# Moving operands split into even and odd tokens, read in turn from both halves

## The chip, the cores and the metric

The kernel runs on one core of a Trainium2 chip. The metric is the device time of one execution in microseconds (us). Before the change three executions took 2588.56, 2589.22 and 2593.65 us, with a median of 2589.22.

The engines are named as in the profile: PE is TensorE (its matmuls) and PEld its weight loads, DVE is VectorE, ACT is ScalarE, POOL is GpSimd, and SP issues most of the DMAs.

## The reference

One layer of a hybrid decoder runs for a prompt of 256 tokens and 8 sample tokens, 264 tokens in all, width 2048. All data is float32. Cut to what matters here:

```python
proj = x @ w_in                        # 2048 -> 15392 columns
z, xbc, dt, sc_b, sc_c, sc_h, g_a, g_b = split(proj)
y_a = ssd_branch(z, xbc, dt, ...)      # causal conv, chunked scan, gated RMS norm
y_b = sc_b * dwconv3(sc_c * sc_h)      # short gated conv
mix = sigmoid(g_a) * (y_a @ w_branch_ssd) + sigmoid(g_b) * (y_b @ w_branch_sc)
x1 = layer_norm(ALPHA * x + mix @ w_out)
# peer: 8 heads, each picks 16 of 16384 experts by product keys
q = x1 @ peer_wq
idx, gate = top-16 per head
hid = gelu(x1 . peer_u[idx])
x2 = layer_norm(ALPHA * x1 + sum(gate * hid * peer_v[idx]))
y = x2 + sigmoid(x2 @ ple_gate_w) * (p @ ple_proj_w)
```

The time goes into products of a weight matrix with the 264 tokens. For the experts the kernel multiplies 208 of the tokens with all 16384 rows of `peer_u` and `peer_v` (the picks are a mask of gates), and gathers rows for the other 56.

## The kernel before

**Layout.** Activations are held transposed: a tile has 128 features as partitions and the tokens as columns, so a product over 2048 features is a sum over 16 tiles (`kb`). The weights are the stationary operand, 128x128 at a time; the tokens are the moving operand and stream through. Results land in PSUM in the order in which the moving columns were read.

**Three products for float32.** Every operand is cut into a high part, rounded to the matmul's input type (float32r), and a low part, the rest. `half_mm` (lines 242 to 244) then adds high weight x high token, high x low and low x high into the same PSUM columns. Weights arrive by DMA in tiles of 128x2048 (`w`, three buffers). ACT makes the high part of each half (`whi`, line 158) and DVE the low part (`wlo`, line 159).

**Column blocks.** `col_block` makes 128 output features of all tokens: two halves of 8 tiles, 48 matmuls of 264 columns. After each half it runs background tasks (`tick`). There are 200 such blocks: 24 for xbc, 48 for the short conv, 16 for z, 32 for each of the two gated branches with their gates, 16 for `w_out`, 16 for the peer queries and 16 for the ple gate. The last two kinds read 266 columns: behind the tokens lie a column of the norm's scale and one of its offset, so that the norm can be applied after the product (`Norm`, tiles `r1` and `r`).

**Pairs.** For the experts, `pair_block` holds the high and low part of 208 tokens in one tile of 416 columns. The high weights meet all 416 at once (lines 278 and 281), the low weights only the first 208 (line 279). So a 128x128 piece of weights costs one wide and one narrow matmul. There are 128 such blocks for `peer_u` (moving tiles `x1`) and 128 for `peer_v` (moving tiles `co`).

**Who makes the moving tiles.** `split_later` (lines 229 and 230) cuts the outputs of the branches (`yb`, `ya`) and their mix (`mx`). `split_x` cuts the input, `Norm.gather` and `Norm.rest` the inputs of the two later col blocks with a norm, `Norm.parts` the 416-wide `x1`, and `prep` (lines 1432 and 1433) the coefficients `co`. Each is one ACT and one DVE instruction per tile. `xsum` (line 1010) adds the two parts of x for the residual, and `residual` (line 1478) copies the `x1` pairs into the accumulators of the second experts' product.

**Order.** Every engine works through its instructions in the order written by the Python program; there is no scheduler. Background work is put between halves by the credits that a task yields.

Of the kernel before, what the change touches and what calls it, by code (L numbers as in the profile page):

```python
# [10 lines left out]
F = mybir.dt.float32  # L11
# [9 lines left out]
T = PT + NS  # L21
# [30 lines left out]
def hybrid_step(ctx: ExitStack, tc: tile.TileContext, xT, pT, w_in, w_dt, w_bs, w_bc, w_o, w_q, w_pg, w_pp,  # L52
# [165 lines left out]
    def run_out(tk):  # L218
        while tk in tasks:
            tick(1e9)  # L220

    def split_later(src, name, new, hs, ls):
        h = new(name + "h", R)
        l = new(name + "l", R)
        hs.append(h)
        ls.append(l)

        def parts():
            ac.copy(h, src)
            ve.tensor_tensor(l, src, h.bitcast(F), OP.subtract)  # L230

        soon(parts)
        return h, l
# [3 lines left out]
    def half_mm(ps, i, kbs, xh, xl, first, last, m=128):  # L237
        hi, lo = his[i], los[i]
        n = len(kbs)
        for q, kb in enumerate(kbs):  # L240
            wh, wl = hi[:, q * 128:q * 128 + m], lo[:, q * 128:q * 128 + m]
            te.matmul(ps, wh, xh[kb], start=(first and q == 0), stop=False)  # L242
            te.matmul(ps, wh, xl[kb], start=False, stop=False)  # L243
            te.matmul(ps, wl, xh[kb], start=False, stop=(last and q == n - 1))  # L244

    def next_half():
        i = pos["i"]
# [20 lines left out]
    def pair_block(xp, evac, budget):  # L268

        ps = psum.tile([128, 512], F, name="mm", tag="mm", bufs=4)[:, :2 * TD]  # L270
        for half in range(2):
            i = next_half()
            hi, lo = his[i], los[i]
            for q in range(8):
                kb = half * 8 + q
                ws = slice(q * 128, q * 128 + 128)
                if kb < KB - 1:
                    te.matmul(ps, hi[:, ws], xp[kb], start=(kb == 0), stop=False)  # L278
                te.matmul(ps[:, :TD], lo[:, ws], xp[kb][:, :TD], start=False, stop=False)  # L279
                if kb == KB - 1:  # L280
                    te.matmul(ps, hi[:, ws], xp[kb], start=False, stop=True)  # L281
            done_half(i)
            if half == 1:
                evac(ps)
            tick(budget)
# [80 lines left out]
    def dt_mm(k0, k1):  # L366
        for kb in range(k0, k1):
            sl = slice(kb * 32, kb * 32 + 32)
            te.matmul(psd[:32, :T], wdh[:, sl], x_h[kb], start=(kb == 0), stop=False)
            te.matmul(psd[:32, :T], wdh[:, sl], x_l[kb], start=False, stop=False)  # L370
            te.matmul(psd[:32, :T], wdl[:, sl], x_h[kb], start=False, stop=(kb == KB - 1))


    wps = bank("warm")
# [467 lines left out]
    class Norm:  # L842
# [24 lines left out]
        def gather(self, s):  # L867

            j = len(self.d)
            w = self.w  # L870
            beside = w < T
            ve.tensor_tensor(s[:, :w], s[:, :w], self.c[:, :w], OP.subtract)
            self.d.append(s[:, :T])
            h, l = self.new(self.name)
            q = s[:, w:2 * w] if beside else block("dsq")

            def on_act():
                ac.activation(h[:, :w], s[:, :w], AF.Copy, scale=col(self.g, j))
                ac.activation(q, s[:, :w], AF.Square)
                gp.tensor_copy(h[:, T:], self.gb[0][:, j])  # L880
                gp.tensor_copy(l[:, T:], self.gb[1][:, j])
                if j == 0:
                    if beside:
                        a = lp.tile([128, 2, w], F, name="da", tag="as", bufs=2)
                        gp.tensor_copy(a.rearrange("p a t -> p (a t)"), s)
                        self.acc = [(a[:, 0], a[:, 1])]
                        self.both = a.rearrange("p a t -> p (a t)")
                    else:
                        a = block("da")
                        gp.tensor_copy(a, s)  # L890
                        self.acc = [(a, q)]

            def on_dve():
                ve.scalar_tensor_tensor(l[:, :w], s[:, :w], col(self.g, j), h[:, :w].bitcast(F), OP.mult, OP.subtract)
# [12 lines left out]
        def rest(self, xs, sq):  # L907
# [19 lines left out]
            for j in range(16):  # L927
                while self.n <= j:
                    yield ("w", 1)
                h, l, x = self.h[j][:, w:T], self.l[j][:, w:T], xs[:, j]  # L930
                ac.activation(h, x, AF.Copy, scale=col(self.g, j))
                gp.tensor_copy(self.d[j][:, w:], x)
# [56 lines left out]
        def parts(self, xp):  # L989
            for j in range(16):  # L990
                d = self.normal(j, ve)
                pr = pair("x1")
                h, l = pr[:, 0:TD], pr[:, TD:2 * TD]
                xp.append(pr[:, 0:2 * TD])

                def split(d=d, h=h, l=l, j=j):
                    ac.copy(h, d[:, :TD])
                    ve.tensor_tensor(l, d[:, :TD], h.bitcast(F), OP.subtract)
                    gp.tensor_copy(x1sp[:, j], d[:, TD:])

                soon(split)
# [411 lines left out]
    def prep(c):  # L1413

        for k in range(4 * c, 4 * c + 4):
# [16 lines left out]
            ac.copy(co[:, :, 0], al)  # L1432
            ve.tensor_tensor(co[:, :, 1], al, co[:, :, 0].bitcast(F), OP.subtract)
            for e in range(4):
                CO[4 * k + e] = co[:, e].rearrange("p a t -> p (a t)")
            yield 1.1
            yield ("w", 2)

# [90 lines left out]
    def ple_half(q):  # L1529
        i = next_half()  # L1530
        hi, lo = his[i], los[i]
        for c in range(4):
            ps = psum.tile([128, TW], F, name="mm", tag="mm", bufs=4)[:, :T]
            for kb in range(2):
                sl = slice((c * 2 + kb) * 128, (c * 2 + kb) * 128 + 128)
                te.matmul(ps, hi[:, sl], p_h[kb], start=(kb == 0), stop=False)
                te.matmul(ps, hi[:, sl], p_l[kb], start=False, stop=False)
                te.matmul(ps, lo[:, sl], p_h[kb], start=False, stop=(kb == 1))
# [61 lines left out]
def _inputs(x_prompt, x_sample, p_prompt, p_sample, state_ssm, state_ssd_conv, state_shortconv,  # L1600
# [71 lines left out]
```

## Time and profile before

| | |
|---|---|
| median of three runs | 2589.22 us |
| the profiled execution: its time | 2585.9 us |
| its span in the trace | 2584.1 us |
| granted TensorE clock, mean | 0.995 |
| PE busy | 2558.3 us, 99% |
| DVE busy | 2041.8 us, 79% |
| ACT busy | 1432.3 us, 55% |
| POOL busy | 602.5 us, 23% |
| moved by DMA | 688.90 MB, mean 267 GB/s |

The program's stages follow each other on PE: the col blocks to about 1145 us, `peer_u` from there to 1833 us, `peer_v` to 2463 us (first and last matmul of lines 278 and 279), then the ple products and the last col blocks.

How to read the rows that follow. A row of the timeline gives the start and the duration of an instruction in us, engine, line, operation, and output and inputs by the program's tile names. For matmuls `128*128` is the size of the weights and `128x264` the moving operand. Matmuls overlap in the pipeline, so their pace is the distance from one start to the next, not their duration. A row of the groups gives the count behind `x`, the busy time in us, the mean duration in ns, and the idle time before them with what ended it. A row of a single line gives the shortest, median and longest duration in ns. A row of the waits says who waited for whom: us in total, times, longest. A row of the windows gives, for a stretch of the span, each engine's busy us, then the granted clock, the DMA engines' share, and GB/s.

### The profile page before, as it was taken

To read this page: it belongs to the slowest core of one execution; us is meant where nothing else is said; L and a number is where in the kernel's file an instruction comes from. 1 tells how busy PE (TensorE), PEld (TensorE's weight loads), DVE (VectorE), ACT (ScalarE), POOL (GpSimd) and SP (SyncE) were. 2 spreads that over 40 slices of the span, in tenths; PEclk is the share of its full clock that TensorE was granted. 3 is DMA by queue.
4 is the path that set the end of the run, shared out by engine and by line. 5 is a ranking of instruction groups with operands and counts; after the bars stand their busy time and mean duration, and the time that the engine had idled before them with its cause. 6 is when DMAs were issued, how large, how long until landed. Compare 5 with 4: busy or idle time off the path is not lost.

```text
span 2584.1 us, 47957 instructions
## 1 busy us (share of the span) xinstructions
PE 2558.3 (99%) x19049; PEld 2537.6 (98%) x19049; DVE 2041.8 (79%) x3296; ACT 1432.3 (55%) x2206; POOL 602.5 (23%) x720
## 2 busy tenths in 40 slices
PE   9999999999999999999999999999999999999999
PEld 8999999999999999999999999999999999999999
DVE  7899965557445557889999877777899998989986
ACT  5665543445334444655577888865544455444563
POOL 2332200000000010100047666543232223322210
PEclk9999999999999999999999999999999999999999
DMA  6788755555555555556669999999999999999553
GB/s 226 228 292 276 251 177 175 182 180 179 181 180 180 180 180 180 177 182 211 226 246 361 362 359 358 354 356 381 377 381 382 368 379 369 373 350 353 205 189 123
DMA packets 137104, 688.90 MB, mean 267 GB/s; under 512 B 15744, under 2 KB 53168, under 8 KB 63280
## 3 DMA queue, kind: packets, MB, share of 16 engines
q1 hardware_dynamic: 89168, 495.46, 53.7%
q0 software_dynamic: 28688, 158.69, 16.0%
q10 hardware_dynamic: 19024, 31.69, 3.3%
q8 instruction: 149, 2.44, 0.4%
q14 instruction: 75, 0.61, 0.1%
HBM read 646.32 MB, written 39.46 MB: 265 GB/s over the span
## 4 chain that ended last, share of the span: by engine, by line
PE 85%; DVE 7%; issue 3%; DMA 3%; ACT 2%; ACTq 0%; POOL 0%; SPq 0%; DVEq 0%; POOLq 0%
PE mm L278 23%; PE mm L244 15%; PE mm L242 15%; PE mm L243 14%; PE mm L279 12%; DVE wlo L159 3%; PE mm L281 2%; PE gps L1263 1%; DMA w<-uT 1%; ACT whi L158 1%; DVE ug L1344 0%; ACT o L1251 0%; DVE as L1389 0%; DMA w<-vP 0%; DMA h0t<-h 0%
## 5 line engine op out<-in xcount | busy, mean ns | idle before, releaser
L159 DVE TENSOR_TENSOR wlo<-w,whi 128x1024 fp32r<-128x1024 f32 x916 | 1114.2, 1222 | 391.6 <-ACT whi L158 389.0
L158 ACT CAST whi<-w 128x1024 fp32r<-128x1024 f32 x916 | 955.8, 1049 | 736.4 <-PE mm L243 283.9
L278 PE MATMUL mm<-x,whi 128*128 128x416 f32 x1920 | 594.3, 370 | 1.4 <-ACT whi L158 1.4
L278 PE MATMUL mm<-co,whi 128*128 128x416 f32 x1920 | 586.1, 367 | 0.0
L244 PE MATMUL mm<-x,wlo 128*128 128x264 f32 x1920 | 549.0, 286 | 4.8 <-DVE wlo L159 4.8
L242 PE MATMUL mm<-x,whi 128*128 128x264 f32 x1920 | 548.1, 285 | 0.0
L243 PE MATMUL mm<-x,whi 128*128 128x264 f32 x1920 | 545.9, 284 | 0.0
L279 PE MATMUL mm<-x,wlo 128*128 128x208 f32 x2048 | 511.0, 260 | 3.9 <-DVE wlo L159 3.8
L279 PE MATMUL mm<-co,wlo 128*128 128x208 f32 x2048 | 509.4, 259 | 0.5 <-DVE wlo L159 0.4
L279 PEld LDWEIGHTS mm<-x,wlo 128*128 128x128 f32 x2048 | 391.9, 191 | 7.2 <-DVE wlo L159 6.8
L279 PEld LDWEIGHTS mm<-co,wlo 128*128 128x128 f32 x2048 | 390.3, 191 | 1.5 <-DVE wlo L159 1.1
L244 PEld LDWEIGHTS mm<-x,wlo 128*128 128x128 f32 x1920 | 362.1, 189 | 5.9 <-DVE wlo L159 5.8
L278 PEld LDWEIGHTS mm<-x,whi 128*128 128x128 f32 x1920 | 362.4, 189 | 5.0 <-ACT whi L158 1.6
L242 PEld LDWEIGHTS mm<-x,whi 128*128 128x128 f32 x1920 | 362.7, 189 | 1.4 <-issue 1.4
L278 PEld LDWEIGHTS mm<-co,whi 128*128 128x128 f32 x1920 | 360.7, 188 | 2.6
L243 PEld LDWEIGHTS mm<-x,whi 128*128 128x128 f32 x1920 | 361.8, 188 | 0.0
L1250 POOL TENSOR_SCALAR o<-iot,slot,slot 128x128 f32<-128x128 f32 x156 | 189.9, 1224 | 3.7 <-issue 2.0
L1274 POOL DMA_INDIRECT ug<-vR,sidx x56 | 98.1, 1752 | 294.9 <-DVE x1s L1354 236.8
L1274 POOL DMA_INDIRECT ug<-uR,sidx x56 | 92.9, 1658 | 269.2 <-DVE ug L1344 231.9
L1344 DVE SCALAR_TENSOR_TENSOR ug<-ug,x1s 128x2048 f32<-128x2048 f32 x56 | 128.0, 2286 | 2.7 <-DMA ug<-uR,sidx 2.7
L1354 DVE SCALAR_TENSOR_TENSOR x1s<-ug,scf,x1s 128x2048 f32<-128x2048 f32 x53 | 124.2, 2344 | 0.2 <-DMA ug<-vR,sidx 0.2
L880 POOL CAST r1h<-r1gbh 128x2 fp32r<-128x2 f32 x16 | 4.4, 278 | 476.0 <-PE mm L244 476.0
(364 smaller groups left out, 3955.9 us busy)
## 6 DMA issues: line engine op xcount, KB each, us to landing
w<-uT SPq DMA_DIRECT2D x128, 1024.0 KB, 6.4
w<-vP SPq DMA_DIRECT2D x128, 1024.0 KB, 8.4
w<-w_in SPq DMA_DIRECT2D x118, 1024.0 KB, 5.0
w<-w_bc SPq DMA_DIRECT2D x16, 1024.0 KB, 4.8
w<-w_bs SPq DMA_DIRECT2D x16, 1024.0 KB, 4.9
w<-w_o SPq DMA_DIRECT2D x16, 1024.0 KB, 4.9
w<-w_q SPq DMA_DIRECT2D x16, 1024.0 KB, 4.8
w<-w_pg SPq DMA_DIRECT2D x16, 1024.0 KB, 4.9
```

The source lines that it names most:

```text
L158: ac.copy(hi, w)
L159: ve.tensor_tensor(lo, w, hi.bitcast(F), OP.subtract)
L242: te.matmul(ps, wh, xh[kb], start=(first and q == 0), stop=False)
L243: te.matmul(ps, wh, xl[kb], start=False, stop=False)
L244: te.matmul(ps, wl, xh[kb], start=False, stop=(last and q == n - 1))
L278: te.matmul(ps, hi[:, ws], xp[kb], start=(kb == 0), stop=False)
L279: te.matmul(ps[:, :TD], lo[:, ws], xp[kb][:, :TD], start=False, stop=False)
L281: te.matmul(ps, hi[:, ws], xp[kb], start=False, stop=True)
L1250: (gp if q < 3 else ve).tensor_scalar(o1[:, q], iot, slot[0][:, c], slot[2][:, c], OP.is_equal, OP.mult)
L1274: gp.indirect_dma_start(out=t, out_offset=None, in_=tab, in_offset=bass.IndirectOffsetOnAxis(ap=sidx[:, c:c + 1], axis=0))
L1344: ve.scalar_tensor_tensor(t, t, 1.0, x1s, OP.mult, OP.mult, accum_out=shid[:, c:c + 1])
L1354: ve.scalar_tensor_tensor(x1s, t, scf[:, c:c + 1], x1s, OP.mult, OP.add)
```

## The change

Every moving tile now holds its tokens with the even ones in front and the odd ones behind: token 2t stands at column t, token 2t + 1 at column t plus half the width. The matmuls read such a tile in turn: first column of the front half, first of the back half, second of the front, and so on (`in_turn`). The results so come out in token order, and nothing that reads PSUM changes. With 264 columns the halves are 132 columns apart, with 266 they are 133 apart (the scale and offset columns stand at the end of each half). In the pairs a half of 208 columns holds 104 high parts and 104 low parts, so the halves are 208 apart for the wide and for the narrow matmul.

The ACT and DVE instructions that make the tiles read every second column (`even_odd`) and write the two halves (`halves`). The input x and the ple input p are permuted before the launch. Every engine has the same instructions as before, in the same order; only the shapes of their operands differ.

```diff
+    def halves(ap):
+        return ap.rearrange("p (a t) -> p a t", a=2)
+    def even_odd(ap):
+        return ap.rearrange("p (t a) -> p a t", a=2)
+    def in_turn(ap):
+        return ap.rearrange("p (a t) -> p t a", a=2)
...
-            ac.copy(h, src)
-            ve.tensor_tensor(l, src, h.bitcast(F), OP.subtract)
+            ac.copy(halves(h), even_odd(src))
+            ve.tensor_tensor(halves(l), even_odd(src), halves(h.bitcast(F)), OP.subtract)
...
-            te.matmul(ps, wh, xh[kb], start=(first and q == 0), stop=False)
-            te.matmul(ps, wh, xl[kb], start=False, stop=False)
-            te.matmul(ps, wl, xh[kb], start=False, stop=(last and q == n - 1))
+            vh, vl = in_turn(xh[kb]), in_turn(xl[kb])
+            te.matmul(ps, wh, vh, start=(first and q == 0), stop=False)
+            te.matmul(ps, wh, vl, start=False, stop=False)
+            te.matmul(ps, wl, vh, start=False, stop=(last and q == n - 1))
...
+                both = in_turn(xp[kb])
+                one = xp[kb].rearrange("p (a o t) -> p o t a", a=2, o=2)[:, 0]
                 if kb < KB - 1:
-                    te.matmul(ps, hi[:, ws], xp[kb], start=(kb == 0), stop=False)
-                te.matmul(ps[:, :TD], lo[:, ws], xp[kb][:, :TD], start=False, stop=False)
+                    te.matmul(ps, hi[:, ws], both, start=(kb == 0), stop=False)
+                te.matmul(ps[:, :TD], lo[:, ws], one, start=False, stop=False)
...
-                ac.activation(h[:, :w], s[:, :w], AF.Copy, scale=col(self.g, j))
+                ac.activation(hv, sv, AF.Copy, scale=col(self.g, j))
...
-                h, l = pr[:, 0:TD], pr[:, TD:2 * TD]
+                pv = pr[:, 0:2 * TD].rearrange("p (a o t) -> p a o t", a=2, o=2)
+                h, l = pv[:, :, 0], pv[:, :, 1]
...
-        ve.tensor_tensor(t, h[j].bitcast(F), l[j].bitcast(F), OP.add)
+        ve.tensor_tensor(even_odd(t), halves(h[j].bitcast(F)), halves(l[j].bitcast(F)), OP.add)
...
-            co = co.rearrange("p (e a t) -> p e a t", e=4, a=2)
-            ac.copy(co[:, :, 0], al)
-            ve.tensor_tensor(co[:, :, 1], al, co[:, :, 0].bitcast(F), OP.subtract)
+            co = co.rearrange("p (e a o t) -> p e a o t", e=4, a=2, o=2)
+            ah = al.rearrange("p e (t a) -> p e a t", a=2)
+            ac.copy(co[:, :, :, 0], ah)
+            ve.tensor_tensor(co[:, :, :, 1], ah, co[:, :, :, 0].bitcast(F), OP.subtract)
...
-            ac.copy(t, x1_p[db].bitcast(F))
+            ac.copy(t.rearrange("p (o t a) -> p o a t", o=2, a=2),
+                    x1_p[db].bitcast(F).rearrange("p (a o t) -> p o a t", a=2, o=2))
...
+    turn = np.arange(T).reshape(T // 2, 2).T.reshape(-1)
-        xT=x.T.reshape(16, 128, T).transpose(1, 0, 2),
-        pT=p.T.reshape(2, 128, T).transpose(1, 0, 2),
+        xT=x[turn].T.reshape(16, 128, T).transpose(1, 0, 2),
+        pT=p[turn].T.reshape(2, 128, T).transpose(1, 0, 2),
```

The three matmuls of the dt columns and of the ple products are changed as those of `half_mm`.

More of the change, by code (lines that the diff above doesn't have):

```diff
@@ L276, in pair_block @@
                 ws = slice(q * 128, q * 128 + 128)
+                both = in_turn(xp[kb])
+                one = xp[kb].rearrange("p (a o t) -> p o t a", a=2, o=2)[:, 0]
                 if kb < KB - 1:
-                    te.matmul(ps, hi[:, ws], xp[kb], start=(kb == 0), stop=False)
-                te.matmul(ps[:, :TD], lo[:, ws], xp[kb][:, :TD], start=False, stop=False)
+                    te.matmul(ps, hi[:, ws], both, start=(kb == 0), stop=False)
+                te.matmul(ps[:, :TD], lo[:, ws], one, start=False, stop=False)
                 if kb == KB - 1:
-                    te.matmul(ps, hi[:, ws], xp[kb], start=False, stop=True)
+                    te.matmul(ps, hi[:, ws], both, start=False, stop=True)
             done_half(i)
@@ L368, in dt_mm @@
             sl = slice(kb * 32, kb * 32 + 32)
-            te.matmul(psd[:32, :T], wdh[:, sl], x_h[kb], start=(kb == 0), stop=False)
-            te.matmul(psd[:32, :T], wdh[:, sl], x_l[kb], start=False, stop=False)
-            te.matmul(psd[:32, :T], wdl[:, sl], x_h[kb], start=False, stop=(kb == KB - 1))
+            vh, vl = in_turn(x_h[kb]), in_turn(x_l[kb])
+            te.matmul(psd[:32, :T], wdh[:, sl], vh, start=(kb == 0), stop=False)
+            te.matmul(psd[:32, :T], wdh[:, sl], vl, start=False, stop=False)
+            te.matmul(psd[:32, :T], wdl[:, sl], vh, start=False, stop=(kb == KB - 1))
     wps = bank("warm")
@@ L874, in gather @@
             h, l = self.new(self.name)
+            hv, lv = halves(h)[:, :, :w // 2], halves(l)[:, :, :w // 2]
+            sv = even_odd(s[:, :w])
             q = s[:, w:2 * w] if beside else block("dsq")
             def on_act():
-                ac.activation(h[:, :w], s[:, :w], AF.Copy, scale=col(self.g, j))
+                ac.activation(hv, sv, AF.Copy, scale=col(self.g, j))
                 ac.activation(q, s[:, :w], AF.Square)
-                gp.tensor_copy(h[:, T:], self.gb[0][:, j])
-                gp.tensor_copy(l[:, T:], self.gb[1][:, j])
+                gp.tensor_copy(halves(h)[:, :, T // 2], self.gb[0][:, j])
+                gp.tensor_copy(halves(l)[:, :, T // 2], self.gb[1][:, j])
                 if j == 0:
@@ L893, in on_dve @@
             def on_dve():
-                ve.scalar_tensor_tensor(l[:, :w], s[:, :w], col(self.g, j), h[:, :w].bitcast(F), OP.mult, OP.subtract)
+                ve.scalar_tensor_tensor(lv, sv, col(self.g, j), hv.bitcast(F), OP.mult, OP.subtract)
                 if j and beside:
@@ L929, in rest @@
                     yield ("w", 1)
-                h, l, x = self.h[j][:, w:T], self.l[j][:, w:T], xs[:, j]
+                h, l = (halves(v[j])[:, :, w // 2:T // 2] for v in (self.h, self.l))
+                x = even_odd(xs[:, j])
                 ac.activation(h, x, AF.Copy, scale=col(self.g, j))
-                gp.tensor_copy(self.d[j][:, w:], x)
+                gp.tensor_copy(self.d[j][:, w:], xs[:, j])
                 def low(h=h, l=l, x=x, j=j):
@@ L992, in parts @@
                 pr = pair("x1")
-                h, l = pr[:, 0:TD], pr[:, TD:2 * TD]
+                pv = pr[:, 0:2 * TD].rearrange("p (a o t) -> p a o t", a=2, o=2)
+                h, l = pv[:, :, 0], pv[:, :, 1]
                 xp.append(pr[:, 0:2 * TD])
                 def split(d=d, h=h, l=l, j=j):
-                    ac.copy(h, d[:, :TD])
-                    ve.tensor_tensor(l, d[:, :TD], h.bitcast(F), OP.subtract)
+                    dv = even_odd(d[:, :TD])
+                    ac.copy(h, dv)
+                    ve.tensor_tensor(l, dv, h.bitcast(F), OP.subtract)
                     gp.tensor_copy(x1sp[:, j], d[:, TD:])
@@ L1430, in prep @@
                 co = vp.tile([128, 8 * TD], R, name="co", tag="co", bufs=4)
-            co = co.rearrange("p (e a t) -> p e a t", e=4, a=2)
-            ac.copy(co[:, :, 0], al)
-            ve.tensor_tensor(co[:, :, 1], al, co[:, :, 0].bitcast(F), OP.subtract)
+            flat = co.rearrange("p (e x) -> p e x", e=4)
+            co = co.rearrange("p (e a o t) -> p e a o t", e=4, a=2, o=2)
+            ah = al.rearrange("p e (t a) -> p e a t", a=2)
+            ac.copy(co[:, :, :, 0], ah)
+            ve.tensor_tensor(co[:, :, :, 1], ah, co[:, :, :, 0].bitcast(F), OP.subtract)
             for e in range(4):
-                CO[4 * k + e] = co[:, e].rearrange("p a t -> p (a t)")
+                CO[4 * k + e] = flat[:, e]
             yield 1.1
@@ L1535, in ple_half @@
                 sl = slice((c * 2 + kb) * 128, (c * 2 + kb) * 128 + 128)
-                te.matmul(ps, hi[:, sl], p_h[kb], start=(kb == 0), stop=False)
-                te.matmul(ps, hi[:, sl], p_l[kb], start=False, stop=False)
-                te.matmul(ps, lo[:, sl], p_h[kb], start=False, stop=(kb == 1))
+                vh, vl = in_turn(p_h[kb]), in_turn(p_l[kb])
+                te.matmul(ps, hi[:, sl], vh, start=(kb == 0), stop=False)
+                te.matmul(ps, hi[:, sl], vl, start=False, stop=False)
+                te.matmul(ps, lo[:, sl], vh, start=False, stop=(kb == 1))
             j = 4 * q + c
```

## The prediction, made before the result was known

> **What bounds the kernel now.** I read the page first, then who TensorE waits for, then the timeline of single matmuls in four places, since a busy share says nothing about the pace inside it.
>
> ```profile
> PE 2558.3 (99%) x19049; PEld 2537.6 (98%) x19049; DVE 2041.8 (79%) x3296; ACT 1432.3 (55%) x2206; POOL 602.5 (23%) x720
> PE 85%; DVE 7%; issue 3%; DMA 3%; ACT 2%; ACTq 0%; POOL 0%; SPq 0%; DVEq 0%; POOLq 0%
> ...
> PE mm L244 <- DVE wlo L159: 4.8, 3, 2.4
> PE mm L279 <- DVE wlo L159: 4.2, 5, 1.6
> ```
>
> TensorE is busy for all but 26 us, and its two longest waits sum to 9 us. So the time is the pace of the matmuls, and only what one matmul takes before the next can start is worth anything. Start to start, that is read here (a row: start, duration, both in us; the durations overlap):
>
> ```profile
> 999.83 0.28 PE L244 MATMUL mm<-mxh,wlo 128*128 128x264 f32 x1
> ...
> 1005.95 0.29 PE L243 MATMUL mm<-mxl,whi 128*128 128x264 f32 x1
> ...
> 1099.82 0.29 PE L244 MATMUL mm<-r1h,wlo 128*128 128x266 f32 x1
> ...
> 1102.93 0.28 PE L242 MATMUL mm<-r1h,whi 128*128 128x266 f32 x1
> ...
> 2439.78 0.37 PE L278 MATMUL mm<-co,whi 128*128 128x416 f32 x1
> 2439.98 0.25 PE L279 MATMUL mm<-co,wlo 128*128 128x208 f32 x1
> ...
> 2443.38 0.37 PE L278 MATMUL mm<-co,whi 128*128 128x416 f32 x1
> ```
>
> Between the first two rows lie 50 steps: 6.12 us / 50 = 122.4 ns for 264 columns. The next two are 25 steps apart: 3.11 / 25 = 124.4 ns for 266. The last stretch holds 12 pairs of a wide (416) and a narrow (208) matmul: 3.60 / 12 = 300 ns a pair.
>
> Two other places tell what those prices are made of. At the start the dt columns are multiplied with weights only 32 wide; in the fold near the end 128-wide weights meet 8 moving columns:
>
> ```profile
> 8.10 0.28 PE L370 MATMUL psd<-x,whi 128*32 128x264 f32 x1
> 8.22 0.28 PE L371 MATMUL psd<-x,wlo 128*32 128x264 f32 x1
> ...
> 9.06 0.28 PE L369 MATMUL psd<-x,whi 128*32 128x264 f32 x1
> ...
> 2420.24 0.97 PEld L1315 LDWEIGHTS yS<-fld,x1s 128*128 128x128 f32 x8
> 2421.13 0.19 PEld L278 LDWEIGHTS mm<-co,whi 128*128 128x128 f32 x1
> ...
> 2001.25 0.36 PE L281 MATMUL mm<-co,whi 128*128 128x416 f32 x1
> 2001.45 0.35 PE L278 MATMUL mm<-co,whi 128*128 128x416 f32 x1
> 2001.64 0.26 PE L279 MATMUL mm<-co,wlo 128*128 128x208 f32 x1
> ```
>
> From 8.10 to 9.06 are 8 steps of 120 ns, with a load a quarter as wide: so **the stream** of 264 moving columns takes 120 ns by itself, 0.4545 ns a column. The eight loads at 2420.24 last 0.97 us, a single one 0.19 (the row below), so a load follows a load after (0.97 - 0.19) / 7 = 111 ns, whatever streams beside it. That is **the floor of a full weight load**; I use 112. A wide matmul whose weights came in during the wide one before it (2001.45) needs 0.19 us; 416 x 0.4545 = 189 ns, so the stream's price is the same at both widths. A pair then is the narrow one, whose 208 x 0.4545 = 95 ns hide under the 112 ns load for the next wide one, and the wide one's 189: 301, where the trace has 300. For 264 columns the stream (120) is longer than the load (112), and 2.4 ns come on top that the narrow-weight rows do not have; for 266 it is 120.9 and 3.5. So in every large matmul but the 208-wide, **how fast the moving operand is read is what ends last**, and the change is about just that.
>
> **The change part by part.** The matmul count, their widths, their weights, the instructions of every engine and their order stay as they are; no wait, transfer or queue is moved. What changes is the address order of the moving operand (neighbouring columns now come from two places half a tile apart), and the address order in about 130 pieces of work on ACT and DVE that make those tiles. The first input and the ple input are permuted before the launch and cost nothing here.
>
> The counts:
>
> ```profile
> L244 PE MATMUL mm<-x,wlo 128*128 128x264 f32 x1920 | 549.0, 286 | 4.8 <-DVE wlo L159 4.8
> ...
> L244 PE MATMUL mm<-mxh,wlo 128*128 128x264 f32 x256 | 72.9, 285 | 0.0
> L244 PE MATMUL mm<-yah,wlo 128*128 128x264 f32 x256 | 72.7, 284 | 0.0
> ...
> L244 PE MATMUL mm<-ybh,wlo 128*128 128x264 f32 x256 | 72.7, 284 | 0.0
> ...
> L244 PE MATMUL mm<-r1h,wlo 128*128 128x266 f32 x256 | 73.8, 288 | 0.0
> ...
> L279 PE MATMUL mm<-x,wlo 128*128 128x208 f32 x2048 | 511.0, 260 | 3.9 <-DVE wlo L159 3.8
> L279 PE MATMUL mm<-co,wlo 128*128 128x208 f32 x2048 | 509.4, 259 | 0.5 <-DVE wlo L159 0.4
> ```
>
> Each of the first five stands for three lines: (1920 + 3 x 256) x 3 = 8064 matmuls of 264; 2 x 256 x 3 = 1536 of 266 (r1 and the last norm's r alike); 4096 pairs. At the prices above: 987 + 191 + 1229 = 2407 us of the 2558.
>
> *The stream.* No row of before shows a moving operand read in turn, so its price is bounded. It can get no lower than the load floor for 264 columns (112 / 264 = 0.424 ns a column, 7% under now); above, the nearest rows are strided reads and writes of other engines:
>
> ```profile
> L921 DVE TENSOR_REDUCE da<-x1sp x1: 1894/1894/1894, 2438.9 to 2438.9; 128x56 f32<-128x896 f32 x1
> ...
> L1171 DVE TENSOR_REDUCE sel<-big x18: 403/675/687, 1255.3 to 1434.1; 128x32 f32<-128x512 f32 x16, 64x16 f32<-64x256 f32 x2
> ...
> L1264 ACT COPY gs<-gps x52: 1072/1133/1176, 1307.0 to 1731.8; 128x512 f32<-128x512 f32 x52
> ...
> L1305 ACT COPY x1s<-x1t x12: 569/586/664, 1318.1 to 2152.6; 128x512 f32<-128x512 f32 x12
> ```
>
> L1171 sums lying neighbours: 256 more elements cost 675 - 403 = 272 ns, 1.06 each, so 131 ns are fixed. L921 jumps 224 bytes at every element: (1894 - 131) / 896 = 1.97, 1.85 times as much. L1264 writes with 128 bytes between neighbours and takes 1133 ns where L1305 takes 586, 1.93 times. So the upper end is 1.85 x 0.4545 = 0.84 ns a column.
>
> I take the lower end, 0.424. Two things decide. The contiguous stream's price grows with the columns alone, 120 and 190 ns, where no load binds; so it is the fetching that limits it, and a fetch that always takes neighbours from one spot leaves room for one that spreads them over two. And L921 and L1264 throw away the rest of each spot they touch, while here each half is still walked through in order: every byte near a fetched one is used two columns later. This is an inference, not a row, and the rivals carry what is against it. With it, keeping the 2.4 and 3.5 ns on top of the floor:
>
> - 264: 122.4 to 114.4, 8.0 ns x 8064 = 64.5 us
> - 266: 124.4 to 115.5, 8.9 ns x 1536 = 13.7 us
> - pair: the narrow one stays at 112, the wide one falls to 416 x 0.424 = 176.4, 12.6 ns x 4096 = 51.6 us
>
> The sum is 130 us. [...]
>
> *What is late next.* In the second experts' matrix little room is left beside TensorE:
>
> ```profile
> 1850.00:2400.00 550.00, 549.48 (x3673) 546.08 (x3672) 505.06 (x515) 265.71 (x297) 160.71 (x154) 1.00 0.95 368
> L1433 DVE TENSOR_TENSOR co<-al,co 128x832 fp32r<-128x832 f32 x32 | 32.5, 1016 | 0.5 <-ACT co L1432 0.5
> L230 DVE TENSOR_TENSOR ybl<-ybf,ybh 128x264 fp32r<-128x264 f32 x16 | 6.8, 426 | 0.0
> ```
>
> (PE, PEld, DVE, ACT, POOL busy; clock; DMA share; GB/s.) DVE is at 505 / 550 = 92%, the DMA engines at 95%. A pair 4.2% shorter asks for 96% of DVE and for more bytes a second than DMA now carries at 95% busy. Half of that matrix's 26 us I give back: 13 us. The row-by-row split of its coefficients (L1433, and its ACT copy) now reads every second element. If that cost nothing it hides; at the 1.85 of L921 it adds 0.85 x 32.5 = 28 us to DVE over some 614 us (2048 pairs at 300 ns), DVE reaches 100%, and this matrix's whole 26 us are gone. I take the lower end: its reads are 8 bytes apart, nearer to L1171's 4 than to L921's 224. The other splits (of the kind of L230, three times 16, and the norms') would at worst add 0.36 us each on DVE and ACT beside a col block of 48 x 122.4 = 5.9 us, where both have room.
>
> Sum: 2585.9 of the profiled execution (span 2584.1 and 1.8 around it) - 130 + 13 = 2469; the median of the runs shown is 3.3 above it, so **2472**.
>
> **The rivals.**
>
> *A new place for every column costs a fetch each time* (the other side). Place: the moving read of every large matmul; price 0.84 ns a column. 264 would take 222 ns (+99.4), 266 223 (+99), a pair 175 + 349 = 524 (+224): 801 + 152 + 918 = 1871 us more, 4460. It decides as soon as a column costs over 122.4 / 264 = 0.464 ns, 2% above now. For it: L921 and L1264 on two engines. Against: the two halves are each read in order, and TensorE already takes 4 bytes in 0.4545 ns, where DVE's lying neighbours need 1.06, so its fetch is built otherwise. [...]
>
> *The order does not matter to TensorE.* The 0.4545 ns are then the array's own, and the 2.4 ns on top move by a nanosecond either way. For it: one price at both widths. Against: 264 columns cost 120 with narrow weights and 122.4 with wide ones, so reading does enter. Then only the strided splits are left: 2589 with them hidden, up to 2589 + 28 + 48 x 0.36 (the three times 16 splits, if none of it hid) = 2634.
>
> *Gained in the front, lost among the experts.* The streams get faster, but DVE and DMA hold both experts' matrices at their pace: only 64.5 + 13.7 = 78 us come, 2511. For it: the 95% and 92% above. Against: TensorE waits for neither there now (549 of 550 us busy).
>
> **How the numbers follow.** The forecast has 0.50, the other side 0.20, the order that does not matter 0.15 (of it 0.08 within 0.2%, 0.07 slower by strided work), the gain lost among the experts 0.15. Differences under 0.2% (5 us) cannot be told from none here. So faster 0.50 + 0.15 = 0.65, same 0.08, slower 0.20 + 0.07 = 0.27. The likeliest's own range is 2420 to 2520. At the low end all of the 2.4 and 3.5 ns go too (10.4 x 8064 + 12.4 x 1536 = 103 us), nothing is given back (52 us) and the wide stream gains as much again (about 40): 2395. The high end is the rival without effect at its worst, 2634. What is left out is the other side, 0.20.
>
> **What will show it.** Right: a step of 264 columns at 112 to 116 ns, a pair near 288, L159's share of DVE up since the span shrinks. The 208-wide ones show nothing, since their load hides them. If the rows of the dt columns (narrow weights) are under 112 ns, the stream itself got faster and the load binds; if they stay at 120 while the wide-weight ones fall, it was the 2.4 ns alone. The other side would be seen at once: 200 ns and more a step, DVE and DMA half idle. If steps shrink and the span doesn't, waits of TensorE on L159 or of ACT on the experts' weights will have grown. The forecast is wrong if reading in turn is one fetch a column, or if the column price has nothing to do with fetching.

## The result and the profile after

The changed kernel takes 2489.47 us (median of 4 runs, 2485.39 to 2492.02) where the kernel before takes 2588.89 us beside it (4 runs): a ratio of 0.9612, 95% interval 0.9592 to 0.9633, so 99 us less. The forecast was 2472, in a range of 2395 to 2634. The profiled execution took 2492.0 us, with a span of 2490.2: 93.9 less than the span before.

From the page after, the busy times and the engines' shares of the chain that ended last:

```profile
PE 2429.0 (98%) x19049; PEld 2403.0 (96%) x19049; DVE 2036.4 (82%) x3296; ACT 1424.4 (57%) x2206; POOL 626.2 (25%) x720
PE 61%; DVE 16%; DMA 10%; issue 7%; ACT 5%; POOL 1%; ACTq 0%; SPq 0%; DVEq 0%; POOLq 0%
```

TensorE was idle for 26 us before and is now for 61 (2490.2 - 2429.0), and the chain runs through DVE for 16% of the span where it was 7%. Its waits after (waiter, releaser: us in total, times, longest):

```profile
PE mm L294 <- DVE wlo L159: 17.0, 26, 2.8
PE mm L257 <- DVE wlo L159: 12.3, 11, 3.4
PE mm L1561 <- DVE acc L1482: 7.2, 2, 4.9
PE mm L255 <- ACT whi L158: 4.7, 1, 4.7
PE mm L293 <- ACT whi L158: 4.5, 1, 4.5
```

(L255 to L257 are the three matmuls of the col blocks now, L293, L294 and L296 those of the pairs.) Before, the two waits on `wlo` made 9 us; now they make 29. The steps of the matmuls, in the same four places as in the prediction (start and duration in us):

```profile
7.78 0.28 PE L387 MATMUL psd<-x,wlo 128*32 128x264 f32 x1
...
8.90 0.28 PE L385 MATMUL psd<-x,whi 128*32 128x264 f32 x1
...
851.66 0.28 PE L255 MATMUL mm<-yah,whi 128*128 128x264 f32 x1
...
856.16 0.28 PE L256 MATMUL mm<-x,whi 128*128 128x264 f32 x1
...
1051.91 0.28 PE L255 MATMUL mm<-r1h,whi 128*128 128x266 f32 x1
...
1053.27 0.28 PE L255 MATMUL mm<-r1h,whi 128*128 128x266 f32 x1
...
2344.14 0.36 PE L293 MATMUL mm<-co,whi 128*128 128x416 f32 x1
...
2347.01 0.36 PE L293 MATMUL mm<-co,whi 128*128 128x416 f32 x1
...
2347.61 0.34 PE L293 MATMUL mm<-co,whi 128*128 128x416 f32 x1
2347.79 0.25 PE L294 MATMUL mm<-co,wlo 128*128 128x208 f32 x1
```

The dt matmuls with weights 32 wide make 10 steps in 1.12 us, 112 ns each (120 before). The next two rows are 40 steps apart, 4.50 / 40 = 112.5 ns (122.4). The 266-column ones make 12 steps in 1.36 us, 113.3 ns (124.4). The stretch from 2344.14 to 2347.01 holds 10 pairs: 287 ns (300). The wide matmul at 2347.61 follows a wide one, so its weights came in before, and takes 0.18 us where it took 0.19; the median of all such steps is 176 ns.

At these prices the steps save 9.9 x 8064 + 11.1 x 1536 + 13 x 4096 = 80 + 17 + 53 = 150 us, and 94 came. The other 56 are in the starts of the matmuls: I summed, over each trace, what every step takes beyond the median of its kind. Steps of over 350 ns, which are holes, cost 24.7 us before and 68.9 now; those between 1.25 times the median and 350 ns cost 25.7 and 37.2. That is 44 + 12 = 56 us. By stage the loss is 15 us in the col blocks, 21 in `peer_u`, 15 in `peer_v`, 4 behind it.

Now the windows of before (us; busy time of PE, PEld, DVE, ACT, POOL; granted clock; DMA share; GB/s): the col blocks, the first 105 us of `peer_u`, `peer_u`, `peer_v`, and a short one from the start.

```profile
10.00:1146.00 1136.00, 1131.16 (x9318) 1123.67 (x9316) 792.40 (x1540) 559.72 (x893) 119.71 (x268) 1.00 0.59 199
1146.00:1251.00 105.00, 103.76 (x696) 101.62 (x694) 100.70 (x335) 57.40 (x92) 1.61 (x3) 1.00 0.65 213
...
1145.50:1833.70 688.20, 680.34 (x4612) 672.32 (x4611) 579.19 (x981) 496.04 (x833) 293.27 (x236) 1.00 0.86 320
1833.80:2463.70 629.90, 629.38 (x4214) 625.65 (x4213) 580.14 (x630) 309.55 (x371) 178.13 (x188) 1.00 0.91 351
...
35.00:60.00 25.00, 25.00 (x208) 24.82 (x207) 24.13 (x50) 11.50 (x25) 5.92 (x12) 1.00 0.53 179
```

And those of after, with two short ones from the start and one from within `peer_v`:

```profile
10.00:1076.00 1066.00, 1048.95 (x9306) 1040.20 (x9304) 788.85 (x1531) 560.18 (x889) 122.06 (x267) 1.00 0.63 212
1077.00:1182.00 105.00, 101.95 (x701) 98.44 (x699) 100.63 (x338) 56.78 (x92) 2.09 (x4) 1.00 0.64 211
...
1076.60:1758.30 681.70, 661.26 (x4611) 650.47 (x4611) 580.79 (x986) 491.71 (x832) 309.63 (x237) 0.99 0.87 323
1758.40:2374.50 616.10, 607.56 (x4213) 602.83 (x4212) 574.38 (x625) 303.19 (x368) 183.09 (x186) 1.00 0.93 359
...
35.00:60.00 25.00, 24.16 (x213) 23.75 (x213) 24.17 (x49) 11.49 (x25) 5.92 (x12) 1.00 0.51 175
194.00:199.00 5.00, 5.00 (x24) 5.00 (x25) 5.00 (x25) 2.91 (x5) 0.00 (x0) 0.52 0.21 53
...
1865.00:2075.00 210.00, 209.78 (x1468) 208.99 (x1467) 199.47 (x211) 106.13 (x137) 64.00 (x58) 1.00 0.98 380
```

The col blocks got shorter by 70 us, `peer_u` by only 7 where its half of the pairs' 53 was to be had, `peer_v` by 14. In `peer_u` TensorE idles 20 us of 682 (8 of 688 before). Its first 105 us are telling: DVE was at 100.7 of 105 us already before, when TensorE hardly noticed; now as many instructions of DVE stand against a shorter row of matmuls, DVE is as full as it was, and TensorE stands still for 3 us: 701 matmuls where there were 696, and 105 us at 287 ns a pair would hold 732. The same holds at 35 to 60 us, with DVE at 24.13 of 25 before and 24.17 after, and TensorE at 25.00 and 24.16. But a full DVE does not hold TensorE back by itself. From 1865 to 2075 us it is busy for 199.47 of 210, and TensorE idles for 0.2 us and makes 1468 matmuls, the full new pace. So it should matter what stands in DVE's queue ahead of the low weights, which such a window does not show. Nor is all of it DVE: of TensorE's 20 idle us in `peer_u`, 10.8 are waits for `wlo` (16 of them), 4.5 one wait for `whi`, 5.1 waits of the small products for POOL and DVE.

The row at 194 us shows slow steps without a hole: TensorE is busy for all of 5 us, with a granted clock of 0.52. They stand behind a hole. From the timeline of after, the wait ahead of them and two rows 18 steps apart, the end of one other wait with the row behind it, and a third wait with two rows 4 pairs apart behind it:

```profile
192.59 0.59 PE L255 MATMUL mm<-x,whi 128*128 128x264 f32 x1 [4.67 <-ACT whi L158]
...
194.22 0.43 PE L255 MATMUL mm<-x,whi 128*128 128x264 f32 x1
...
198.18 0.43 PE L255 MATMUL mm<-x,whi 128*128 128x264 f32 x1
...
1183.25 0.36 PE L294 MATMUL mm<-x,wlo 128*128 128x208 f32 x1 [2.78 <-DVE wlo L159]
1183.44 0.36 PE L293 MATMUL mm<-x,whi 128*128 128x416 f32 x1
...
1219.39 0.48 PE L1222 MATMUL slt<-ident,sel 128*128 128x128 f32 x1 [2.38 <-DVE sel L1201]
...
1220.18 0.59 PE L293 MATMUL mm<-x,whi 128*128 128x416 f32 x1
...
1222.42 0.54 PE L293 MATMUL mm<-x,whi 128*128 128x416 f32 x1
```

Behind 4.67 us of idleness a step takes 3.96 / 18 = 220 ns, nearly twice 112.5; behind 2.78 us the narrow step takes 0.19 once and the rest of that stretch is at its usual pace (12 pairs in 3.45 us from 1183.73 on, with a granted clock of 1.00 from 1183.2 to 1190). But it is not only the longer wait that is paid for in this way: behind only 2.38 us of idleness a pair takes 2.24 / 4 = 560 ns, twice its 287, with a granted clock of 0.50 from 1219.4 to 1222.8. So a hole can be paid for twice, and in this trace its length alone does not tell whether it will be.

### The profile page after: what moved, and what is told of

Read it like the earlier page. It is cut to its first block, busy times and chain, and to the rows that moved or that the text cites. A ratio compares the mean times of both kernels' runs of the same rounds, so it can differ in the third digit from the quotient of the medians.

```text
span 2490.2 us, 47970 instructions
## 1 busy us (share of the span) xinstructions
PE 2429.0 (98%) x19049; PEld 2403.0 (96%) x19049; DVE 2036.4 (82%) x3296; ACT 1424.4 (57%) x2206; POOL 626.2 (25%) x720
## 4 chain that ended last, share of the span: by engine, by line
PE 61%; DVE 16%; DMA 10%; issue 7%; ACT 5%; POOL 1%; ACTq 0%; SPq 0%; DVEq 0%; POOLq 0%
PE mm L255 13%; PE mm L257 13%; PE mm L256 13%; PE mm L293 13%; DVE wlo L159 7%; PE mm L294 6%; DMA w<-vP 5%; ACT whi L158 2%; DMA w<-uT 2%; DVE ug L1365 1%; DMA h0t<-h 1%; PE gps L1284 1%; DVE acc L1482 1%; PE mm L296 1%; ACT o L1272 1%
## 5 line engine op out<-in xcount | busy, mean ns | idle before, releaser
L158 ACT CAST whi<-w 128x1024 fp32r<-128x1024 f32 x916 | 945.3, 1044 | 648.1 <-DMA w<-vP 228.6
L293 PE MATMUL mm<-x,whi 128*128 128x416 f32 x1920 | 573.1, 365 | 4.5 <-ACT whi L158 4.5
L293 PE MATMUL mm<-co,whi 128*128 128x416 f32 x1920 | 563.3, 362 | 0.0
L257 PE MATMUL mm<-x,wlo 128*128 128x264 f32 x1920 | 533.4, 278 | 12.4 <-DVE wlo L159 12.3
L255 PE MATMUL mm<-x,whi 128*128 128x264 f32 x1920 | 534.5, 278 | 4.7 <-ACT whi L158 4.7
L256 PE MATMUL mm<-x,whi 128*128 128x264 f32 x1920 | 531.9, 277 | 0.0
L294 PE MATMUL mm<-x,wlo 128*128 128x208 f32 x2048 | 504.6, 257 | 10.9 <-DVE wlo L159 10.8
L294 PE MATMUL mm<-co,wlo 128*128 128x208 f32 x2048 | 501.4, 255 | 6.5 <-DVE wlo L159 6.2
L294 PEld LDWEIGHTS mm<-x,wlo 128*128 128x128 f32 x2048 | 393.2, 193 | 18.9 <-DVE wlo L159 18.1
L294 PEld LDWEIGHTS mm<-co,wlo 128*128 128x128 f32 x2048 | 391.3, 192 | 10.9 <-DVE wlo L159 10.8
L257 PEld LDWEIGHTS mm<-x,wlo 128*128 128x128 f32 x1920 | 364.7, 190 | 15.1 <-DVE wlo L159 15.0
L293 PEld LDWEIGHTS mm<-x,whi 128*128 128x128 f32 x1920 | 365.9, 191 | 6.0 <-ACT whi L158 4.8
L255 PEld LDWEIGHTS mm<-x,whi 128*128 128x128 f32 x1920 | 364.9, 190 | 6.3 <-ACT whi L158 4.9
L293 PEld LDWEIGHTS mm<-co,whi 128*128 128x128 f32 x1920 | 364.0, 190 | 0.1
L1271 POOL TENSOR_SCALAR o<-iot,slot,slot 128x128 f32<-128x128 f32 x156 | 200.8, 1294 | 3.0 <-issue 1.2
L1295 POOL DMA_INDIRECT ug<-vR,sidx x56 | 105.2, 1879 | 271.8 <-DVE x1s L1375 212.8
```

Of the source, the lines that this page charges most:

```text
L158: ac.copy(hi, w)
L255: te.matmul(ps, wh, vh, start=(first and q == 0), stop=False)
L256: te.matmul(ps, wh, vl, start=False, stop=False)
L257: te.matmul(ps, wl, vh, start=False, stop=(last and q == n - 1))
L293: te.matmul(ps, hi[:, ws], both, start=(kb == 0), stop=False)
L294: te.matmul(ps[:, :TD], lo[:, ws], one, start=False, stop=False)
```

## The experiments

### What of the order makes the step shorter

The changed kernel, with other reading orders in the first 72 col blocks and the first 120 pair blocks. Each order is a view of the same tile:

```
halves     "p (a t) -> p t a"         a=2        0 132 1 133 ...
within     "p (b a t) -> p b t a"     a=2, t=2   0 2 1 3 | 4 6 5 7 ...
four       "p (b a t) -> p b t a"     a=2, t=4   0 4 1 5 2 6 3 7 | 8 12 ...
quarters   "p (a t) -> p t a"         a=4        0 66 132 198 1 67 ...
steptwo    "p (t a) -> p a t"         a=2        0 2 4 6 ... then 1 3 5 ...
twotwo     "p (a t u) -> p t a u"     a=2, u=2   0 1 132 133 2 3 ...
```

(`four`, `dozen`, `eight` and `sixteen` have two places that many columns apart, `stepfour` and so on are as `steptwo`, `fourfour` as `twotwo`. Of the second kernel's names in the rows below, `three` has two places 3 columns apart, `wfour` four places 4 apart.)

> The changed kernel, but the first 72 col blocks and the first 120 pair blocks read their moving operand in orders that take turns from block to block (the results land in other token orders there, so the outputs are not the reference's; the work is the same). Read from the steps between matmul starts. Theory 'two spots': two neighbouring columns fetched one after the other from one spot of 16 bytes are what costs; every order whose next column lies in another spot runs at the new pace, 112.5 ns for 264 columns and about 176 for 416 where no weight load binds (a step of 198 in the pairs): halves, four columns apart, eight, sixteen, twelve, quarters, steps of four, eight, twelve. Orders that stay in the spot or come back two at a time (within: 0 2 1 3; steps of two; four and four) stay at 120 to 124 and 205. Rival 'a new place is a fetch': an order that leaves each spot after one column and comes back much later (steps of four, eight, twelve) pays for each column, 220 ns and more for 264, and only those that return soon (halves, quarters, four apart) are fast. Rival 'distance': only far places help, so four and eight columns apart stay at the old pace and halves and quarters do not.

> The changed kernel with other reading orders in the first 72 col blocks and the first 120 pair blocks (the tokens are mixed up, so the outputs aren't the reference's). Orders of two places 3, 6, 22 and 66 columns apart, and of four places 6 and 22 columns apart, six places 4 apart (264 columns); four places 4 and 52 columns apart (416 columns). Theory (it is the number of places that are walked through at once that counts, not how far they lie from each other): two places 112 at 6, 22 and 66 columns apart, at 3 columns between the 122 of two apart and the 112 of four apart; four places slow near as far, about 140 at 264 columns and about 237 at 416. Rival (what costs is that the places lie far from each other, in different pieces of memory): four places 4 columns apart, that is within 16 columns, run as fast as two, 198 at 416 columns, and four places 6 apart near 112, while 22 and 52 apart give 140 and 237.

Median from start to start in ns, of matmuls with 264 columns, and of the wide ones of a pair (416 columns; the narrow one behind it reads from both halves in turn in every row, as in the change):

| order | 264 | 416 |
|---|---|---|
| plain | 122 | 211 |
| two places half a tile apart (halves) | 112 | 198 |
| two places 66 / 22 / 6 apart | 113 / 113 / 113 | |
| two places 16 / 12 / 8 apart | - / 113 / - | 198 / - / 198 |
| two places 4 apart (four) | 112 | 198 |
| two places 3 apart | 141 | |
| two places 2 apart (within) | 122 | 211 |
| four places far apart (quarters) | 142 | 237 |
| four places 22 / 6 apart | 145 / 152 | |
| four places 52 / 4 apart | | 238 / 235 |
| six places 4 apart | 153 | |
| two from each half in turn (twotwo) | 170 | 284 |
| four from each half in turn (fourfour) | 132 | 215 |
| every second (steptwo) | 236 | 359 |
| every fourth / eighth / twelfth | 240 / - / 321 | 357 / 338 / - |

From the timeline of the first of the two kernels, two rows 20 steps apart for each of `four`, `quarters` and `steptwo`:

```profile
36.82 0.28 PE L275 MATMUL four<-x,whi 128*128 128x264 f32 x1
...
39.07 0.28 PE L277 MATMUL four<-x,wlo 128*128 128x264 f32 x1
...
47.70 0.31 PE L275 MATMUL quarters<-x,whi 128*128 128x264 f32 x1
...
50.55 0.31 PE L277 MATMUL quarters<-x,wlo 128*128 128x264 f32 x1
...
54.79 0.42 PE L275 MATMUL steptwo<-x,whi 128*128 128x264 f32 x1
...
59.50 0.43 PE L277 MATMUL steptwo<-x,wlo 128*128 128x264 f32 x1
```

2.25 / 20 = 112.5, 2.85 / 20 = 142.5 and 4.71 / 20 = 235.5 ns. And of the second kernel, 20 steps of two places 3 apart and 12 pairs of four places 4 apart:

```profile
25.68 0.30 PE L279 MATMUL three<-x,whi 128*128 128x264 f32 x1
...
28.50 0.30 PE L281 MATMUL three<-x,wlo 128*128 128x264 f32 x1
...
1125.04 0.40 PE L327 MATMUL wfour<-x,whi 128*128 128x416 f32 x1
...
1128.94 0.40 PE L327 MATMUL wfour<-x,whi 128*128 128x416 f32 x1
```

2.82 / 20 = 141 ns; 3.90 / 12 = 325 ns a pair, where the changed kernel has 287.

Three things follow. From 4 columns (16 bytes) on distance is not it: two places that near do as well as two 132 apart (112 ns both), and four places slow the read whether they lie 4 or 52 columns apart (235 and 238 ns at 416 columns, where two take 198), so the rivals that asked for far places, or for near ones, both fall. Two places at least 4 columns apart, each walked through column by column, are what runs at 112; no other number of places that was tried does. And the rival's price is real in other orders: steps over neighbours cost 236 / 264 = 0.89 to 321 / 264 = 1.22 ns a column, against a forecast of 0.84 for any order that leaves its place. The theory of the first kernel, that every order whose next column lies in another spot runs at the new pace, missed: the four quarters take 142 ns and the steps of four and twelve 240 and 321, where it had 112, and steps of two (236), two and four at a time (170, 132) lie above its 120 to 124. The expectation for 3 apart, between 112 and 122, was missed by far (141); why that order is worse than both its neighbours, and why plain order is slower than two places at all, these runs don't tell.

### The layout and the reading apart

The layout alone (the tiles as in the change, every matmul reads them plainly):

```diff
     def in_turn(ap):
-        return ap.rearrange("p (a t) -> p t a", a=2)
+        return ap
...
-                one = xp[kb].rearrange("p (a o t) -> p o t a", a=2, o=2)[:, 0]
+                one = xp[kb].rearrange("p (a o t) -> p o a t", a=2, o=2)[:, 0]
```

> Tiles laid out with the even tokens in front, as in the change, but read front to back (results in another token order, so the outputs are not the reference's). If the reading order alone is the gain, this has the steps of before (122 and 300 ns a pair) and the time of before plus what the strided ACT and DVE work costs: 2589 to 2605. If the layout or where the tiles lie gave the gain, it is near 2489.

2590.72 us (10 runs) beside 2587.23 for before: ratio 1.0016, 1.0006 to 1.0026. The strided splits alone cost some 4 us, under the 5 that count as a difference.

The reading alone: the kernel before, whose matmuls read in turn from both halves of unpermuted tiles; its tokens come out in another order than the reference's.

```diff
-            te.matmul(ps, wh, xh[kb], start=(first and q == 0), stop=False)
+            vh, vl = in_turn(xh[kb]), in_turn(xl[kb])
+            te.matmul(ps, wh, vh, start=(first and q == 0), stop=False)
...
+                both, one = in_turn(xp[kb]), in_turn(xp[kb][:, :TD])
...
```

> The kernel before with only the reading order changed: tiles in token order, read in turn from both halves (results in another token order, so the outputs are not the reference's). If the reading order alone is the gain and the strided work is hidden: 2489, within 5 us. If the strided work of ACT and DVE costs something in the changed kernel: 2455 to 2480. If the layout matters: near 2589.

2489.17 us, ratio 0.9616, 0.9595 to 0.9638: the change's own time, without any strided work on ACT and DVE. So the reading is all of the gain, and the splits cost nothing that shows. In the changed kernel the costliest of them, by line in the window of `peer_v` (its mean was 1016 ns before):

```profile
L1456 DVE TENSOR_TENSOR co<-al,co 128x832 fp32r<-128x832 f32 x28 | 28.5, 1017 | 0.0
```

The change in the col blocks only, with plain pairs:

```diff
-                both = in_turn(xp[kb])
-                one = xp[kb].rearrange("p (a o t) -> p o t a", a=2, o=2)[:, 0]
+                both = xp[kb]
+                one = xp[kb][:, :TD]
...
```

> The change in the col blocks alone; the expert pairs laid out and read as before. By the sum of the prediction the col blocks give 78 us: 2511. From the stages of the two traces they give 59 + 9 + 8 = 76: 2513. If the pairs' part of the change is worth the 39 us that was forecast, 2528; if pairs in turn and col blocks in turn hinder each other (DVE late among the experts), less than 2513.

2512.62 us, ratio 0.9711, 0.9694 to 0.9727: 75 us from the columns, and the other 23 from the pairs, whose steps are worth 53.

### Who holds what was not gained

DVE's background work made smaller, in the kernel before and in the changed one alike: the top-k searches look at 16 elements in place of the full rows, from the start or after the first eight, and the gathered experts' products at 128 of 2048. The two kernels leave that part of the computation out. One of the edited places:

```diff
...
-                ve.scalar_tensor_tensor(t, t, 1.0, x1s, OP.mult, OP.mult, accum_out=shid[:, c:c + 1])
+                ve.scalar_tensor_tensor(t[:, :128], t[:, :128], 1.0, x1s[:, :128], OP.mult, OP.mult, accum_out=shid[:, c:c + 1])
...
```

> The kernel before with DVE relieved in the experts' stages: the two products of a gathered row (2.3 us each, 112 of them) work on 128 of 2048 columns, and the top-k of the peer heads looks at 16 of 128 keys (results wrong, order and transfers unchanged). Half of a pair with the next one: theory 'DVE holds the pairs' gain back' needs the difference to the changed kernel relieved in the same way. By itself TensorE hardly waited among the experts before (9 us in all), so this is 2575 to 2589 by either theory.

> The changed kernel with the same relief of DVE. The pairs' steps fell by 13 ns, 4096 of them make 53 us, of which the two stages show 20. If DVE (its low parts of the weights queued behind other work) holds back the rest, the difference between the two relieved kernels is 97 + 25 to 33: 122 to 130 us, so this is near 2455. If the transfers of the second experts' stage (95 to 99% busy) or anything else but DVE holds it, the difference stays 97 us and this is near 2480 to 2489.

2578.88 us (ratio 0.9964, 0.9950 to 0.9979) and 2464.59 (0.9523, 0.9507 to 0.9539): 114 us apart, where the unrelieved kernels are 99. So this work on DVE holds some of it, some 15 us, but neither the 122 to 130 of the one theory nor the 97 of the other came out. The windows of `peer_u` and `peer_v`, first of the relieved kernel before:

```profile
1148.00:1828.70 680.70, 677.26 (x4612) 671.30 (x4612) 475.21 (x983) 497.67 (x835) 258.54 (x239) 1.00 0.87 324
1828.80:2457.50 628.70, 628.70 (x4213) 625.55 (x4212) 480.17 (x628) 309.70 (x369) 139.35 (x184) 1.00 0.92 351
```

and of the relieved kernel with the change:

```profile
1074.50:1743.30 668.80, 657.34 (x4611) 649.98 (x4611) 472.28 (x983) 492.69 (x834) 259.22 (x239) 0.99 0.88 329
1743.40:2347.90 604.50, 602.75 (x4213) 601.55 (x4213) 474.62 (x625) 309.08 (x368) 149.01 (x183) 1.00 0.94 365
```

In `peer_v` the change now saves 628.7 - 604.5 = 24 us of the 26.6 that its 2048 pairs are worth, at a DMA share of 0.94: what held it was DVE, not the transfers. In `peer_u` it saves 12 of 26.6. There TensorE still waits 6.4 us for `wlo` (10.8 without the relief), 2.4 us for a small product's input and 2.3 us for `whi`; whether other work on DVE causes the first was not tried.

### The credits of the background work

Three tries to take the holes away by spreading the work otherwise, all from the changed kernel. First fewer credits in the front:

```diff
-        col_block(x_h, x_l, conv_evac(b), 0.9)
+        col_block(x_h, x_l, conv_evac(b), 0.85)
...
-        col_block(x_h, x_l, sc_c(j))
+        col_block(x_h, x_l, sc_c(j), 1.1)
```

(and so for the other two kinds of the short conv, from 1.3 as well.)

> The changed kernel, with less background work allowed after each half in the first 72 col blocks (0.9 to 0.85 for the first 24, 1.3 to 1.1 for the next 48), so that it is spread over more of them. In the changed kernel DVE is 97 to 98% busy from 100 to 300 us and TensorE idles about 13 us there. If DVE's queue is crowded by the credits there, 5 to 12 us come: 2477 to 2484. If the same work is only late elsewhere (the end of that stage waits for it): 2489 or more.

2487.56 us, ratio 0.9604, 0.9588 to 0.9621: no gain to be told from the change's 0.9612. A miss. (DVE is not at 97 to 98% all the way from 100 to 300 us in the changed kernel: from 150 to 200 us it is busy for 44.14 of 50, and the long hole before 192.59 lies there.)

Then fewer among the experts:

```diff
-        pair_block(x1_p, u_evac(e), 1.1)
+        pair_block(x1_p, u_evac(e), 0.95)
...
-            pair_block(co, v_evac(c, db), 1.1)
+            pair_block(co, v_evac(c, db), 0.95)
```

> The changed kernel with 0.95 in place of 1.1 as allowance for background work after each half in both experts' stages. If the low parts of the weights wait on DVE behind background work: 2472 to 2484. If spreading it makes the gates or the coefficients late, TensorE stands still at the change of stages and it is 2495 or more.

2524.28 us, ratio 0.9737, 0.9710 to 0.9764: worse by 35 us. Its windows (the first 105 us of `peer_u`; between the two matrices) and its longest wait:

```profile
1077.00:1182.00 105.00, 105.00 (x734) 103.48 (x733) 100.58 (x322) 56.81 (x93) 1.62 (x3) 1.00 0.67 223
...
1743.00:1760.00 17.00, 0.21 (x2) 0.00 (x0) 8.16 (x9) 6.71 (x11) 5.50 (x8) 0.59 0.86 309
```

```profile
PE mm L293 <- DVE co L1456: 35.6, 5, 17.2
```

With fewer background instructions between the low weights (322 where the change has 338) TensorE is busy for all of the first 105 us, although DVE is as full as in the change (100.58 us), and `peer_u` ends after 668 us instead of 682. But the coefficients are then late: TensorE waits 36 us for them, 17 of these in one hole between the two matrices.

Last, the same sum of credits moved within `peer_u`:

```diff
-        pair_block(x1_p, u_evac(e), 1.1)
+        pair_block(x1_p, u_evac(e), 0.95 if e < 64 else 1.25)
```

> The changed kernel with the credits of background work per half block of peer_u at 0.95 for the first 64 blocks and 1.25 for the other 64 (1.1 throughout before; the sum is the same), all else as in the change. Theory (in peer_u the steps' gain of 26.6 us is lost where VectorE's queue of background work stands ahead of the low weights, which is its first half): peer_u as short as with 0.95 throughout, about 668 to 673 us in place of 681.6, peer_v unchanged at 616, so 2476 to 2482 us, ratio 0.956 to 0.959. Rival (the holes only move: the same work makes the same waits in the later blocks): peer_u at 680, 2487 to 2491 us. Second rival (the gates come late again, as with 0.95 throughout): a hole of some us between the last block of peer_u and the first of peer_v, and no gain.

2496.87 us beside 2585.87, ratio 0.9650, 0.9632 to 0.9669: no gain, rather a loss. `peer_u` fell to 674 us, but `peer_v` grew from 616 to 630, with a wait that the change has not:

```profile
PE mm L293 <- DVE co L1456: 12.9, 3, 7.4
```

So work put off in `peer_u` comes due as late coefficients in `peer_v`. None of the three beats the change. Of what was tried, less work on DVE helped (e6), work moved elsewhere did not.

## Why the prediction was right, and where it was off

**What bounds the kernel: right.** TensorE's pace was the time, and only the steps could be worth something.

**The stream's lower end, 0.424 ns a column: right in size, for a cause put wrongly.** The prediction took the load floor, 112 ns, as the limit. The dt matmuls, with loads a quarter as wide, are at 112 too, so for 264 columns the stream itself ends there. That both limits stand at 112 ns for this width is luck. 416 columns take 176 ns, and the 264, 152 fewer, take 112.5, so (176 - 112.5) / 152 = 0.418 ns a column and 2 ns beside.

**The inference on fetching: half shown.** That the order of reading limits the stream is shown (e3, e1), and that two places are better than one. Why is not: the picture of a fetch that "spreads" the neighbours over two spots has nothing against four, and they take 142. The argument was good enough to pick the right order, and no run shows that it is the reason.

**The 2.4 and 3.5 ns kept on top: wrong.** They went. That is (114.4 - 112.5) x 8064 + (115.5 - 113.3) x 1536 = 15 + 3 = 19 us of the 20 by which the steps' sum of 130 was short; the pairs' 12.6 ns were 13.

**Half of the second experts' matrix given back, 13 us: right there, and far too small for the whole.** `peer_v` gave back 26.6 - 13.8 = 13 us (15 by the sum over its steps), and DVE was its holder as the 92% said, not DMA (e6). The step that failed is that it stopped at `peer_v`: 15 us were lost in the col blocks, 21 in `peer_u`, 4 behind the experts. A row that would have warned of it stands in the trace of before: in the first 105 us of `peer_u` DVE is busy for 100.7. The prediction read a stage's mean (92% in `peer_v`) and did not look for short stretches in which DVE was full, nor at what stands there ahead of `wlo`. With the two errors put right the sum is 2585.9 - 150 + 56 = 2492, the profiled execution's time; they partly cancelled, 20 against 43, so the forecast came out nearer to the measured time than its terms were, by luck.

**The strided splits hidden: right,** and even free for the costliest (1017 ns against 1016).

**The rivals.** A fetch for every column: the price was right, 0.84 forecast, 0.89 measured for every second column and 0.91 (240 / 264) for every fourth, but it does not fall on two places read in turn. No effect: refuted by e2 and e3 together. All lost among the experts, 2511: rather more than half of it happened: e4, which has only the columns, is at 2512.6, and the pairs brought 23 us of their 53.

**What stays open.** Of the 56 us, e6 shows some 15 to be DVE's top-k and gathered experts. The `wlo` waits put 20 us (29 against 9) on DVE's queue as a whole; the part of them in the col blocks was tried by credits alone (e7) without success. Of the 12 us of steps between 1.25 times the median and 350 ns, 3 fall into stretches at half the clock (6.0 us before, 9.0 after), and 4.5 come from the sorting: the last wide matmul of a block (L296) starts 112 ns behind a narrow one as it did before (113), and that only counts as slow now that the median of these steps is 89 and not 96. The two longest waits for `whi` (4.7 and 4.5 us) do not look like DVE's doing: DVE itself waits for `whi` there, 5.36 and 12.67 us. ACT comes to both late, behind a wait for a transfer (timeline of after):

```profile
188.54 0.69 ACT L683 ACTIVATE h0t<-h0t,dexp 128x128 f32<-128x128 f32 x2 [6.22 <-DMA h0t<-h]
...
1676.93 1.01 ACT L1501 COPY acc<-x 128x416 f32<-128x416 f32 x2 [11.35 <-DMA g_d<-gs]
```

The trace of before has the second of these too, at 8.64 us, and TensorE waited 1.4 us behind it. No run takes these transfers out of ACT's way, so that they are the cause is read from the trace and not shown.

## What to carry to other kernels

Where TensorE is busy for nearly all of the span, work out its price for a column from two widths of the moving operand; if float32 columns read in order cost more than the 0.418 ns of this case, try the same read from two places in turn. Here 4 columns between them were enough (112 ns for 264 columns, against 122 in plain order), 2 and 3 were too few (122 and 141), and four places were worse than one (142 to 152). Before adding up a faster step, look at windows of some 100 us for the engine that feeds it: one that is full there, though at 80% over the span, may keep what the step saves. It is a warning and no more, since at 1865 to 2075 us DVE is 95% busy and keeps nothing; look at what its queue holds ahead of the feeding work. Moving that work brought nothing in three tries here, less of it brought 15 us.

## What was not expected of the hardware

A contiguous float32 moving operand is not the fastest: 0.4545 ns a column, against 0.418 for two places in turn; 264 columns take 120 and 112 ns with narrow weights, 122 and 112.5 with wide ones. Two places 3 columns apart take 141 ns where 2 apart take 122 and 4 apart 112. Four places in turn are slower than plain order, 142 to 152 ns. And a DVE instruction that reads 832 elements in an order of every second one took as long as with neighbours, 1017 and 1016 ns.
